# Memory values projected in the cross layers instead of beside the scans of the first mixers, in a two-model FP32 kernel on one core

## The chip, the cores and the metric

The kernel runs on one core of one Trainium2 chip. The metric is the device time of one execution in microseconds (us), the median of several runs. TensorE is called PE, VectorE DVE, ScalarE ACT, GpSimd POOL; SyncE, here SP, issues the DMA transfers of the main queue.

## The reference, cut to what matters

Two models of two layers each stand one behind the other, on 512 tokens of width 1024. In the first each layer is a mixer (attention beside a gated delta rule, which is scanned over chunks of 64 tokens in both directions) and a feed-forward block. In the second each layer is a mixer (even, odd), a cross attention to a memory of 256 rows, and a feed-forward block. The memory is an input and doesn't depend on the tokens:

```python
def _memory_cross_attention(h, mem_h, w_q, w_kv, q_norm_g, k_norm_g, w_o):
    q = _rms(_split_heads(h @ w_q, XA_HEADS), q_norm_g)          # 4 heads of 256
    mk, mv = _split_cols(mem_h @ w_kv, (XA_HEADS * XA_HD, XA_HEADS * XA_HD))
    mk = _rms(_split_heads(mk, XA_HEADS), k_norm_g)
    mv = _split_heads(mv, XA_HEADS)
    logits = jnp.einsum('bhqd,bhkd->bhqk', q, mk) * (XA_HD ** -0.5)
    p = jax.nn.softmax(logits, axis=-1)
    o = jnp.einsum('bhqk,bhkd->bhqd', p, mv)
    return _merge_heads(o) @ w_o

...
        x = x + _memory_cross_attention(_rms(x, xa_norm_g[l]), _rms(mem, xa_mem_norm_g[l]), ...)
```

`mem_h @ w_kv`, the keys and values of the memory, is what the change moves.

## The kernel before, in words

Ten phases follow each other: m0 f0 m1 f1 (the first model's mixers and feed-forward blocks), ev xa0 g0 od xa1 g1 (the second's mixers, cross attentions and feed-forward blocks). A framework with a scheduler takes the program as written and decides the order of the instructions on each engine; SP takes its transfers in that order, one behind another, and each waits on SP until its buffer is free or its data are there.

Every large product is made of three matmuls on split numbers: high part of the weights by high part of the activation (L491), high by low (L494), low by high (L495), in `proj`. Weights come by 1024 KB transfers (`fetch`, L465, two buffers `wraw`), and are split a piece at a time: ACT makes `whi` (L478), POOL `wlo` (L384, a line that all helpers' additions share).

The scan of a mixer (`scan`, `scan_step`) has 16 steps, which alternate between the two directions. A step is a chain: products with `kes` (L1202), an addition on DVE (`yv`), products with `invs`, a multiplication on DVE, products with `keys`, the new state `S` on DVE, and products with `outs` (L1236). The tiles `kes`, `keys`, `outs` come from DRAM in units that serve two steps (`load`, L1151 to L1154); `invs` come by `join` (L1161), which finishes the inverse blocks with two groups of matmuls (L1173, L1180) and copies on ACT (`offd`, L1165; `prod`).

Beside the scan runs side work, a chain of generators: first what is left of the gate logits (blocks of 24 matmuls of 512 columns), then `memory_kv(l, last)`, then the attention's output products. `side.beside(scan(), R3)` lets the scan do a step, which counts 4.0, and runs side work until its own count reaches R3 times the steps' count. Each half group of `memory_kv` counts 3 and is 24 matmuls of 256 columns; with R3 = 0.75 that is one half group a step. `memory_kv` of layer l (l = 0 in m0, 1 in m1) reads the memory, scales and splits it into four `act` tiles, and then for each of four heads projects the keys (two half groups, through `proj`) and the values (two half groups, L1677, L1680 and L1681), copies them on ACT and writes them to DRAM (`mkv`, eight transfers of 256 KB per layer, L1686). `issue_behind` lets such a block start only behind the scan's last L1236 matmul of that moment.

The cross layer (`_cross`) projects the queries of a head (`queries`: 48 matmuls of 512 columns), reads that head's keys and values back (`ahead`, L1722), norms the keys (a sum by L416, a spread over partitions by L459, `kn`), scales the values on ACT, and makes the logits (L1754 to L1756), the softmax and the products with the values (L1781 to L1783).

Of the kernel before, what the change touches and what calls it, by code (L numbers as in the profile page):

```python
# [251 lines left out]

R1, R2, R3, R4 = 0.6,1,0.75,0.6
G1, G2 = 0, 2
E1, E2 = 0,3

# [47 lines left out]
class Prog:  # L306
# [1337 lines left out]
    def memory_kv(self, l, last):  # L1644


        nc, M, wkv = self.nc, NMEM, self.A["xakv"][l]
        mem = self.fetch(self.A["mem"], 8, M)
        ma = []
        for k in range(8):  # L1650
            if k % 2 == 0:
                t = self.actp.tile([P, 2, 2, M], F32R, name="act", tag="act")
            a, g = t[:, k % 2], self.vec(f"xm{l}", k)
            nc.scalar.activation(a[:, 0], mem[:, k], AF.Copy, scale=g)
            nc.vector.scalar_tensor_tensor(a[:, 1], mem[:, k], g, a[:, 0].bitcast(F32), ALU.mult, ALU.subtract)
            ma.append(a)
        for h in range(4):
            for g in (h, 4 + h):
                ws = self.wload(wkv[g], 8, 256, rows=g > 3)
                t = self.nrm.tile([P, 2, M], F32, name="mkv", tag="nsq", bufs=2)  # L1660
                dst = self.dr.tile([P, 2, M], F32, name=f"mkv{l}{g}")
                self.mkv[l, g] = dst
                if g < 4:
                    for j in range(2):
                        ps = self.psb()[:, :M]
                        self.proj(ps, ws[j], ma, n=M, behind=last[-1] if last else None)
                        nc.scalar.copy(t[:, j], ps)
                        if j == 0:
                            yield 3
                else:  # L1670
                    pv = [self.psb()[:, :M] for _ in range(2)]
                    for i, (k0, hi, lo) in enumerate(ws[0]):
                        for j in range(2):
                            tok = slice(j * P, (j + 1) * P)
                            for k in range(2):
                                a = ma[k0 + k]
                                mm = nc.tensor.matmul(pv[j], a[:, 0, tok], hi[:, k], start=k0 + k == 0, stop=False)  # L1677
                                if last and k + j == 0 and i % 2 == 0:
                                    self.issue_behind(mm, last[-1])
                                nc.tensor.matmul(pv[j], a[:, 0, tok], lo[:, k], start=False, stop=False)  # L1680
                                nc.tensor.matmul(pv[j], a[:, 1, tok], hi[:, k], start=False, stop=k0 + k == 7)  # L1681
                        if i == 1:
                            yield 3
                    for j in range(2):
                        nc.scalar.copy(t[:, j], pv[j])
                nc.sync.dma_start(out=dst, in_=t)  # L1686
                yield 3

    def cross(self, l, nm, nxt):
        with self.phase("xa") as xp, self.banks(2, 2, 2):  # L1690
# [2 lines left out]
    def _cross(self, l, nm, nxt, xp):  # L1693
        nc, gs = self.nc, self.gs
        wq = self.A["xaq"][l]
        M = NMEM

        def roots(sq, scale, eps, n, r):

            self.tt(sq[0], sq[0], sq[1], ALU.add, "gpsimd")  # L1700
            return self.rs_cols([sq[0]], self.all_features, 1, scale, eps, nt=n // P, r=r)[0]

        def queries(h):

            qs, sqs = [], []
            for i, w in enumerate(self.wload(wq[h], 8, 256)):
                ps, q, sq, g = self.psb(), gs("qs", 4, (P, 2, S), F32R), gs("sq", 4), self.vec(f"xq{l}", i)
                self.proj(ps, w, nm.acts)
                nc.scalar.activation(q[:, 0], ps, AF.Copy, scale=g)
                nc.vector.scalar_tensor_tensor(q[:, 1], ps, g, q[:, 0].bitcast(F32), ALU.mult, ALU.subtract)  # L1710
                nc.scalar.activation(sq, ps, AF.Square)
                qs.append(q)
                sqs.append(sq)
            return qs, roots(sqs, 1.0, 256 * EPS, S, nm)


        mr = self.mem[l]
        q0 = queries(0)

        def ahead(g):  # L1720
            t = gs("mkv", 4, (P, 2, M))
            nc.sync.dma_start(out=t, in_=self.mkv[l, g])  # L1722
            return t

        ys = []
        for h in range(4):
            kr, vr = ahead(h), ahead(4 + h)
            kn, ks, sqs = [], [], []
            for j in range(2):
                x, sq = gs("kx", 3, (P, M)), gs("sq", 4)[:, :M]  # L1730
                nc.scalar.activation(x, kr[:, j], AF.Copy, scale=self.vec(f"xk{l}", j))
                nc.scalar.activation(sq, kr[:, j], AF.Square)
                ks.append(x)
                sqs.append(sq)
            ps = self.spread(roots(sqs, 1.0 / 256, EPS, M, mr), nt=2)[:, :M]
            for x in ks:
                self.tt(x, x, ps, ALU.mult)
                kn.append(gs("kn", 4, (P, 2, M), F32R))
                self.split(kn[-1], x)
            vt = [gs("vt", 4, (P, 2, M), F32R) for _ in range(2)]  # L1740
            for t in range(2):
                v = gs("kx", 3, (P, M))
                nc.scalar.activation(v, vr[:, t], AF.Copy, scale=mr.rc[:, t])
                self.split(vt[t], v, "gpsimd")
            qs, rq = q0 if h == 0 else queries(h)

            pT = [gs("pT", 3, (P, 2, S), F32R) for _ in range(2)]
            for q2 in range(2):
                ps = self.psf()
                for t in range(2):  # L1750
                    tk, o = slice((2 * q2 + t) * P, (2 * q2 + t) * P + P), ps[:, t * M:t * M + M]
                    for i in range(2):
                        a, b = qs[i], kn[i]
                        nc.tensor.matmul(o, a[:, 0, tk], b[:, 0], start=i == 0, stop=False)  # L1754
                        nc.tensor.matmul(o, a[:, 0, tk], b[:, 1], start=False, stop=False)  # L1755
                        nc.tensor.matmul(o, a[:, 1, tk], b[:, 0], start=False, stop=i == 1)  # L1756
                pt = self.psg()
                mx = xp.tile([P, 4], F32, name="mx", tag="mx", bufs=4)
                nc.vector.tensor_reduce(mx[:, 0:2], ps.rearrange("p (t m) -> p t m", t=2), AX.X, ALU.max, negate=True)
                pr = gs("pr", 2)  # L1760
                tq = rq[:, 2 * q2:2 * q2 + 2].rearrange("p t c -> p (t c)")
                self.tt(mx[:, 0:2], mx[:, 0:2], tq, ALU.mult)
                for t in range(2):
                    p = pr[:, t * M:t * M + M]
                    nc.scalar.activation(p, ps[:, t * M:t * M + M], AF.Exp, bias=mx[:, t:t + 1], scale=tq[:, t:t + 1],
                                         accum_out=mx[:, 2 + t:3 + t])
                nc.vector.reciprocal(mx[:, 2:4], mx[:, 2:4])
                for t in range(2):
                    p = pr[:, t * M:t * M + M]
                    nc.vector.tensor_scalar(p, p, mx[:, 2 + t:3 + t], None, ALU.mult)  # L1770
                    for k in range(2):
                        nc.tensor.transpose(pt[:, (2 * k + t) * P:(2 * k + t + 1) * P], p[:, k * P:(k + 1) * P], self.ident)  # L1772
                pv = pt.rearrange("p (k t) -> p k t", k=2)
                tk = slice(q2 * 256, q2 * 256 + 256)
                nc.scalar.copy(pT[0][:, :, tk], pv)
                self.tt(pT[1][:, :, tk], pv, pT[0][:, :, tk].bitcast(F32), ALU.subtract)
            for i in range(2):
                po = self.psg()
                c = slice(i * P, i * P + P)
                for k in range(2):  # L1780
                    nc.tensor.matmul(po, vt[k][:, 0, c], pT[0][:, k], start=k == 0, stop=False)  # L1781
                    nc.tensor.matmul(po, vt[k][:, 1, c], pT[0][:, k], start=False, stop=False)  # L1782
                    nc.tensor.matmul(po, vt[k][:, 0, c], pT[1][:, k], start=False, stop=k == 1)  # L1783
                y = xp.tile([P, 2, S], F32R, name=f"y{2 * h + i}")
                self.split(y, po)
                ys.append(y)
        self.out_proj(self.A["xao"][l], ys[:4], nxt, final=False)
        self.out_proj(self.A["xao"][l], ys[4:], nxt, 4)
# [45 lines left out]
```

## Time and profile before

| | |
|---|---|
| median of 3 runs | 3359.07 us (3357.63 to 3361.22) |
| the profiled execution's own time | 3360.63 us |
| its span in the trace | 3358.8 us |
| PE busy | 3211.1 us, 96% of the span |
| DVE, ACT, POOL busy | 54%, 45%, 51% |
| mean granted TensorE clock | 0.987 of full speed |
| scans of the mixers | about 344 to 450 us and 1250 to 1356 us |
| first parts of the cross layers | about 2137 to 2182 us and 2880 to 2920 us |

PE busy is the engine that nearly always works. The 147.6 us in which it doesn't lie in a few stages, the two scans and the starts of the cross layers among them. A line of the trace's order shows start, length, engine, source line, operation, output and inputs; what stands in square brackets is the idle time of the engine just before the instruction, and what ended it.

### The profile page before, as it was taken

The page shows a single profiled execution, that of the slowest core. Times are in us where ns is not written, and L with a number is a line of the kernel's source. Part 1 is how long each engine was busy: PE and PEld are TensorE (multiplying, and loading weights), DVE is VectorE, ACT ScalarE, POOL GpSimd, SP SyncE. Part 2 cuts the span into 40 slices and gives each one's busy share as a digit, 9 for nine tenths or more (in the row PEclk, how much of TensorE's full clock was granted, in tenths as well). Part 3 has the DMA queues.
Part 4 walks back from the last instruction along what each step waited for, and adds up shares of the span by engine and source line. Part 5 has one row for each costly group of instructions (what it writes and reads, how often), then busy time and mean ns, then how long its engine had stood idle before and what let it go on. Part 6 is the DMA issues. An engine that isn't in the chain of part 4 may idle for free. (4 is left out here: it accounts for less than half of the span.)

```text
span 3358.8 us, 47110 instructions
## 1 busy us (share of the span) xinstructions
PE 3211.1 (96%) x17342; PEld 2647.7 (79%) x17342; DVE 1822.8 (54%) x3549; ACT 1512.8 (45%) x2836; POOL 1721.8 (51%) x1453
## 2 busy tenths in 40 slices
PE   8988899999998898999999999899999999999999
PEld 6767787888886677878888777687888888888887
DVE  7687444734476964456445667673232476653222
ACT  5646544433455555344334433554343444644332
POOL 4542466444545334755445555645555533555554
PEclk9999999999999999999999999999999999999999
DMA  4632643222337236422222211323222221222222
GB/s 156 175 98 65 171 142 122 96 101 101 115 110 198 82 92 179 140 100 97 92 101 104 86 63 51 101 75 119 103 101 88 100 81 59 97 90 92 99 101 88
DMA packets 142301, 355.13 MB, mean 106 GB/s; under 512 B 44111, under 2 KB 81359, under 8 KB 113144
## 3 DMA queue, kind: packets, MB, share of 16 engines
q1 hardware_dynamic: 140640, 348.63, 32.4%
q10 hardware_dynamic: 1432, 3.49, 0.4%
q8 instruction: 138, 2.26, 0.3%
q14 instruction: 91, 0.75, 0.1%
HBM read 318.44 MB, written 34.16 MB: 105 GB/s over the span
## 5 line engine op out<-in xcount | busy, mean ns | idle before, releaser
L384 POOL TENSOR_TENSOR wlo<-wraw,whi 128x512 fp32r<-128x512 f32 (+2 forms) x1044 | 1353.4, 1299 | 1412.7 <-ACT whi L478 1359.4
L478 ACT CAST whi<-wraw 128x512 fp32r<-128x512 f32 (+2 forms) x1044 | 633.1, 608 | 1120.8 <-PE psb L494 816.6
L491 PE MATMUL psb<-act,whi 128*128 128x512 f32 (+1 forms) x2016 | 788.5, 392 | 26.0 <-ACT whi L478 12.7
L495 PE MATMUL psb<-act,wlo 128*128 128x512 f32 (+1 forms) x2016 | 782.8, 389 | 0.8 <-POOL wlo L384 0.6
L494 PE MATMUL psb<-act,whi 128*128 128x512 f32 (+1 forms) x2016 | 782.7, 388 | 0.6 <-DVE act L277 0.6
L491 PEld LDWEIGHTS psb<-act,whi 128*128 128x128 f32 x2016 | 383.4, 190 | 105.2 <-ACT whi L478 14.6
L495 PEld LDWEIGHTS psb<-act,wlo 128*128 128x128 f32 x2016 | 382.6, 190 | 76.5 <-POOL wlo L384 2.8
L494 PEld LDWEIGHTS psb<-act,whi 128*128 128x128 f32 x2016 | 383.3, 190 | 74.4 <-DVE act L277 1.9
L384 DVE TENSOR_TENSOR x<-psb,x 128x512 f32<-128x512 f32 x168 | 115.2, 689 | 372.5 <-PE psb L495 372.1
L491 PE MATMUL ps<-act,whi 128*128 128x512 f32 (+1 forms) x720 | 282.4, 392 | 3.4 <-ACT rB L303 3.4
L494 PE MATMUL ps<-act,whi 128*128 128x512 f32 (+1 forms) x720 | 281.8, 391 | 0.0
L495 PE MATMUL ps<-act,wlo 128*128 128x512 f32 (+1 forms) x720 | 281.4, 391 | 0.0
L491 PE MATMUL psb<-mid,whi 128*128 128x512 f32 x704 | 276.5, 394 | 1.0 <-DVE x L384 1.0
L495 PE MATMUL psb<-mid,wlo 128*128 128x512 f32 x704 | 276.2, 392 | 0.0
L494 PE MATMUL psb<-mid,whi 128*128 128x512 f32 x704 | 273.7, 389 | 0.0
L491 PEld LDWEIGHTS ps<-act,whi 128*128 128x128 f32 (+1 forms) x720 | 134.8, 187 | 34.2 <-ACT rB L303 4.7
L495 PEld LDWEIGHTS ps<-act,wlo 128*128 128x128 f32 (+1 forms) x720 | 134.9, 187 | 29.7
L494 PEld LDWEIGHTS ps<-act,whi 128*128 128x128 f32 (+1 forms) x720 | 134.9, 187 | 29.4
L495 PEld LDWEIGHTS psb<-mid,wlo 128*128 128x128 f32 x704 | 132.2, 188 | 30.3
L491 PEld LDWEIGHTS psb<-mid,whi 128*128 128x128 f32 x704 | 132.3, 188 | 29.4 <-DVE x L384 1.5
L494 PEld LDWEIGHTS psb<-mid,whi 128*128 128x128 f32 x704 | 132.1, 188 | 29.6
L384 DVE TENSOR_TENSOR cv<-ps,cv 128x512 f32<-128x512 f32 (+1 forms) x60 | 41.5, 692 | 187.9 <-PE ps L495 106.5
(427 smaller groups left out, 5268.1 us busy)
## 6 DMA issues: line engine op xcount, KB each, us to landing
wraw<-in_wup SPq DMA_DIRECT2D x44, 1024.0 KB, 4.8
wraw<-in_fup SPq DMA_DIRECT2D x44, 1024.0 KB, 4.9
wraw<-in_win SPq DMA_DIRECT2D x38, 1024.0 KB, 5.1
wraw<-in_xakv SPq DMA_DIRECT2D x16, 1024.0 KB, 7.1
wraw<-in_wdn SPq DMA_DIRECT2D x16, 1024.0 KB, 4.8
wraw<-in_evin SPq DMA_DIRECT2D x16, 1024.0 KB, 4.8
wraw<-in_fdn SPq DMA_DIRECT2D x16, 1024.0 KB, 4.9
wraw<-in_odin SPq DMA_DIRECT2D x12, 1024.0 KB, 4.8
```

The lines of the kernel that those rows point to most:

```text
L384: getattr(self.nc, eng).tensor_tensor(out, a, b, op)
L478: nc.scalar.copy(hi, part)
L491: mm = nc.tensor.matmul(ps, hi[:, i], acts[k][:, 0, :n], start=k == 0, stop=False)
L494: nc.tensor.matmul(ps, hi[:, i], acts[k][:, 1, :n], start=False, stop=False)
L495: nc.tensor.matmul(ps, lo[:, i], acts[k][:, 0, :n], start=False, stop=k == kc - 1)
```

## The change

R3 falls from 0.75 to 0.375, so that a half group stands at every second step, and `memory_kv` makes only the keys: 8 half groups of 24 matmuls per layer in place of 16. The four split tiles of the memory, which it made already, are also written to DRAM (`mact`, 4 times 512 KB per layer). The cross layer reads these four tiles back, and for each head fetches and splits the value weights (1024 KB) and makes the 48 value matmuls there, into two PSUM banks, from which ACT takes them with the scale. The values' way through DRAM (4 writes and 4 reads of 256 KB per layer) and their 8 ACT copies per layer are gone.

```diff
-R1, R2, R3, R4 = 0.6,1,0.75,0.6
+R1, R2, R3, R4 = 0.6,1,0.375,0.6
@@ memory_kv
+        self.mkv[l] = parts = self.dr.tile([4, P, 2, 2, M], F32, name=f"mact{l}")
...
             ma.append(a)
+            if k % 2:
+                nc.sync.dma_start(out=parts[k // 2], in_=t.bitcast(F32))
         for h in range(4):
-            for g in (h, 4 + h):
-                ws = self.wload(wkv[g], 8, 256, rows=g > 3)
...
-                else:
-                    pv = [self.psb()[:, :M] for _ in range(2)]
-                    for i, (k0, hi, lo) in enumerate(ws[0]):
-                        for j in range(2):
...
-                    for j in range(2):
-                        nc.scalar.copy(t[:, j], pv[j])
-                nc.sync.dma_start(out=dst, in_=t)
-                yield 3
+            ws = self.wload(wkv[h], 8, 256)
+            t = self.nrm.tile([P, 2, M], F32, name="mkv", tag="nsq", bufs=2)
+            self.mkv[l, h] = dst = self.dr.tile([P, 2, M], F32, name=f"mkv{l}{h}")
+            for j in range(2):
+                ps = self.psb()[:, :M]
+                self.proj(ps, ws[j], ma, n=M, behind=last[-1] if last else None)
+                nc.scalar.copy(t[:, j], ps)
+                if j == 0:
+                    yield 3
+            nc.sync.dma_start(out=dst, in_=t)
+            yield 3
@@ _cross
         mr = self.mem[l]
+        wkv = self.A["xakv"][l]
+        mt = [gs("mact", 4, (P, 2, 2, M), F32R) for k in range(4)]
+        for k in range(4):
+            nc.sync.dma_start(out=mt[k].bitcast(F32), in_=self.mkv[l][k])
+        ma = [mt[k // 2][:, k % 2] for k in range(8)]
         q0 = queries(0)
...
-            kr, vr = ahead(h), ahead(4 + h)
+            kr = ahead(h)
...
+            ws = self.wload(wkv[4 + h], 8, 256, rows=True)
             vt = [gs("vt", 4, (P, 2, M), F32R) for _ in range(2)]
+            pv = [self.psb() for _ in range(2)]
             for t in range(2):
+                tok = slice(t * P, (t + 1) * P)
+                o = pv[t][:, :M]
+                for k, hi, lo in ws[0]:
+                    for i in range(2):
+                        nc.tensor.matmul(o, ma[k + i][:, 0, tok], hi[:, i], start=k + i == 0, stop=False)
+                        nc.tensor.matmul(o, ma[k + i][:, 0, tok], lo[:, i], start=False, stop=False)
+                        nc.tensor.matmul(o, ma[k + i][:, 1, tok], hi[:, i], start=False, stop=k + i == 7)
                 v = gs("kx", 3, (P, M))
-                nc.scalar.activation(v, vr[:, t], AF.Copy, scale=mr.rc[:, t])
+                nc.scalar.activation(v, o, AF.Copy, scale=mr.rc[:, t])
```

What the scheduler makes of it is seen in the engines' order. On PE in the scan of m0 a step with a half group behind it stood so before (the four groups of a step, then the first two of the half group's 24 matmuls):

```order
L1202 MATMUL ps_3833<-yv,invs_3247 64x64 x8
L1202 MATMUL ps_3896<-S,kes_3243 64x64 x8
L1202 MATMUL ps_3848<-yv,keys_3246 64x64 x8
L1236 MATMUL ps_3858<-sv_3819,outs_3251 64x64 x8
L491 MATMUL psb<-act,whi 128x256
L494 MATMUL psb<-act,whi 128x256
```

After the change there is at this place (behind the last block of gate logits) no block for four steps:

```order
L1202 MATMUL ps_3814<-yv,invs_3249 64x64 x8
L1202 MATMUL ps_3889<-S,kes_3244 64x64 x8
L1202 MATMUL ps_3829<-yv,keys_3245 64x64 x8
L1236 MATMUL ps_3839<-sv_3800,outs_3250 64x64 x8
L1202 MATMUL ps_3902<-yv,invs_3247 64x64 x8
L1202 MATMUL ps_3975<-S,kes_3243 64x64 x8
L1202 MATMUL ps_3917<-yv,keys_3246 64x64 x8
L1236 MATMUL ps_3927<-sv_3888,outs_3251 64x64 x8
```

Over the whole scan 11 half groups stood between steps and 5 behind the last step; now 4 stand between steps, one in two steps, and 4 behind the last. The third block of gate logits stands two steps later than before.

On SP in the same scan, behind the loads of the fourth unit, there stood before, with the units' loads around two fetches of memory weights:

```order
L1161 DMA invs_3248<-ti_198 64x8x64 x2
L465 DMA wraw<-in_xakv 128x2048
L1154 DMA keys_3246<-scrK 64x4x128
L1152 DMA outs_3251<-dnscr 128x8x128
L1154 DMA keys_3246<-scrK 64x4x128
L465 DMA wraw<-in_xakv 128x2048
L1151 DMA kes_3243<-dnscr 64x4x128 x2
```

and now:

```order
L1161 DMA invs_3248<-ti_198 64x8x64 x2
L1659 DMA mact_4025<-act 128x1024 x4
L465 DMA wraw<-in_xakv 128x2048
L1151 DMA kes_3243<-dnscr 64x4x128 x2
L465 DMA wraw<-in_xakv 128x2048
L1161 DMA invs_3249<-ti_201 64x8x64 x2
L1151 DMA kes_3244<-dnscr 64x4x128
```

The four writes of the memory's tiles and the first weight fetch stand ahead of the fifth unit's `kes`; the second fetch stands ahead of the next `invs`.

On PE in cross layer 0 the last query matmul was followed by the keys' spread (L459) and the logits (L1754, with `kn` the normed keys and `qs` the queries):

```order
L495 MATMUL psb<-act,wlo 128x512
L459 MATMUL ps_19740<-cstt,rc 128x128 x2
L416 MATMUL ps_19856<-cstt,sq 128x128 x2
L1754 MATMUL ps_19763<-kn,qs 128x256
```

and now there are 96 value matmuls of the heads 0 and 1 (L1737 to L1739 in the changed kernel) ahead of that spread, of which these are the last two (L1752 is now the first line of the logits):

```order
L1738 MATMUL psb<-wlo,mact 128x256
L1739 MATMUL psb<-whi,mact 128x256
L459 MATMUL ps_19172<-cstt,rc 128x128 x2
L416 MATMUL ps_19354<-cstt,sq 128x128 x2
L1752 MATMUL ps_19263<-kn,qs 128x256
```

The values of heads 2 and 3 stand between the later logits and query products. In cross layer 1 it is alike. In m1, ahead of the scan, the scheduler's order changes too, with no edit there: 21 projection matmuls of 512 columns more (141 in place of 120) stand ahead of the last transposes (L864) that feed the inversion (`solve`).

## Rows read from the trace of the kernel before

**Rows 1.** Page, busy time of the engines: span, and PE's busy time.

```profile
span 3358.8 us, 47110 instructions
PE 3211.1 (96%) x17342; PEld 2647.7 (79%) x17342; DVE 1822.8 (54%) x3549; ACT 1512.8 (45%) x2836; POOL 1721.8 (51%) x1453
```

**Rows 2.** Scans by stretch: length, busy by engine, then clock, DMA share, GB/s.

```profile
core 0: us, PE busy (x) PEld busy (x) DVE busy (x) ACT busy (x) POOL busy (x), PEclk, DMA share, GB/s
344.00:380.00 36.00, 30.81 (x483) 26.44 (x484) 20.23 (x50) 21.28 (x52) 12.66 (x21) 0.91 0.58 160
357.00:364.20 7.20, 5.38 (x146) 4.66 (x144) 5.84 (x15) 2.33 (x5) 1.90 (x2) 1.00 0.22 58
380.00:410.00 30.00, 26.28 (x449) 23.58 (x447) 11.25 (x30) 15.20 (x37) 14.57 (x18) 1.00 0.72 185
...
1250.00:1286.00 36.00, 29.42 (x492) 24.68 (x492) 20.47 (x51) 22.64 (x57) 13.56 (x22) 1.00 0.61 168
```

**Rows 3.** PE in order of time, m0's scan, a step without a block.

```profile
360.01 0.69 PE L1202 MATMUL ps<-yv,keys 128*64 128x64 f32 x16 [1.22 <-DVE yv L384]
...
362.62 0.69 PE L1202 MATMUL ps<-yv,keys 128*64 128x64 f32 x16
363.60 0.69 PE L1236 MATMUL ps<-sv,outs 128*64 128x64 f32 x16 [0.29 <-DVE sv L384]
```

**Rows 4.** PE in order of time, m0's scan, a step with a half group.

```profile
386.10 0.69 PE L1236 MATMUL ps<-sv,outs 128*64 128x64 f32 x16 [0.25 <-PE ps L1202]
386.71 0.38 PE L491 MATMUL psb<-act,whi 128*128 128x256 f32 x1
...
389.56 0.28 PE L495 MATMUL psb<-act,wlo 128*128 128x256 f32 x1
389.77 0.69 PE L1202 MATMUL ps<-yv,invs 128*64 128x64 f32 x16
...
391.99 0.69 PE L1236 MATMUL ps<-sv,outs 128*64 128x64 f32 x16 [0.30 <-DVE sv L384]
```

**Rows 5.** PE in order of time, m0's scan, the wait for a late inverse block.

```profile
406.31 0.69 PE L1173 MATMUL ps<-invs,offd 128*64 128x64 f32 x16 [2.83 <-ACT offd L1165]
```

**Rows 6.** DMA issues, 340 to 460 us: transfer, count, KB each, us to landing.

```profile
wraw<-in_xakv SPq DMA_DIRECT2D x8, 1024.0 KB, 8.3
outs<-dnscr SPq DMA_DIRECT2D x6, 512.0 KB, 6.6
mkv<-mkv SPq DMA_DIRECT2D x7, 256.0 KB, 2.0
```

**Rows 7.** DMA issues of the whole span, from the page: an undisturbed weight fetch.

```profile
wraw<-in_wup SPq DMA_DIRECT2D x44, 1024.0 KB, 4.8
```

**Rows 8.** Cross layers by stretch, columns as in the scans.

```profile
2137.00:2160.00 23.00, 22.95 (x108) 19.05 (x108) 11.79 (x22) 15.60 (x32) 21.02 (x18) 1.00 0.50 165
2160.00:2182.00 22.00, 18.11 (x95) 15.29 (x94) 14.58 (x63) 12.47 (x30) 10.07 (x10) 0.95 0.23 72
...
2900.00:2920.00 20.00, 17.86 (x100) 15.31 (x99) 15.79 (x68) 12.46 (x31) 7.28 (x7) 0.91 0.17 52
```

**Rows 9.** Waits in cross layer 0: us in total, times, longest.

```profile
PE ps L459 <- DVE rc L384: 2.7, 1, 2.7
```

**Rows 10.** Line 384, 2130 to 2185 us: pieces of low weights on POOL, ns min/median/max.

```profile
L384 POOL TENSOR_TENSOR wlo<-wraw,whi x17: 1189/1290/1743, 2131.7 to 2172.7; 128x512 fp32r<-128x512 f32 x16, 128x256 fp32r<-128x256 f32 x1
```

**Rows 11.** SP in order of time, cross layer 0: the reads of keys and values.

```profile
2137.13 1.75 SPq L1722 DMA_DIRECT2D mkv<-mkv  x4
2143.93 0.33 SPq L465 DMA_DIRECT2D wraw<-in_xaq  x1
```

**Rows 12.** Mixer m1 ahead of its scan, by stretch, around the inversion.

```profile
1050.00:1110.00 60.00, 46.82 (x205) 37.34 (x204) 37.13 (x69) 21.00 (x40) 26.47 (x22) 0.89 0.64 172
1110.00:1170.00 60.00, 51.42 (x249) 39.91 (x248) 55.36 (x113) 32.84 (x64) 21.17 (x15) 0.97 0.35 93
```

**Rows 13.** Waits in m1, 1020 to 1175 us: us in total, times, longest.

```profile
PE ps L416 <- ACT cv L884: 7.5, 1, 7.5
```

**Rows 14.** A stretch of f0 with nothing but matmuls of 512 columns on PE.

```profile
540.00:560.00 20.00, 20.00 (x88) 16.05 (x87) 6.26 (x8) 9.34 (x15) 13.56 (x22) 1.00 0.21 76
```

More of the change, by code (lines that the diff above doesn't have):

```diff
@@ L1656, in memory_kv @@
             ma.append(a)
+            if k % 2:
+                nc.sync.dma_start(out=parts[k // 2], in_=t.bitcast(F32))
         for h in range(4):
-            for g in (h, 4 + h):
-                ws = self.wload(wkv[g], 8, 256, rows=g > 3)
[L1660 to L1663, printed above, removed]
-                    for j in range(2):
[L1665 to L1668, printed above, removed]
-                            yield 3
-                else:
-                    pv = [self.psb()[:, :M] for _ in range(2)]
-                    for i, (k0, hi, lo) in enumerate(ws[0]):
-                        for j in range(2):
[L1674 to L1684, printed above, removed]
-                        nc.scalar.copy(t[:, j], pv[j])
-                nc.sync.dma_start(out=dst, in_=t)
-                yield 3
@@ L1717, in _cross @@
         mr = self.mem[l]
+        wkv = self.A["xakv"][l]
[3 more added lines that the diff above has]
+        ma = [mt[k // 2][:, k % 2] for k in range(8)]
         q0 = queries(0)
         def ahead(g):
-            t = gs("mkv", 4, (P, 2, M))
+            t = gs("mkv", 2, (P, 2, M))
             nc.sync.dma_start(out=t, in_=self.mkv[l, g])
```

## The prediction

> **What bounds the kernel now.** I begin with the page: PE is busy for 3211.1 of 3358.8 us [rows 1]. The reader should see that 147.6 us are all that can be won by better order, and that the 384 value matmuls which the change moves (192 per layer) are neither saved nor added. So the question is only how much PE time is idle or slow around them, in the place that they leave and in the place to which they go.
>
> The second view is the scans by stretch [rows 2]. From 344 to 380 us PE is idle for 5.2 of 36 us, and from 380 to 410 for 3.7 of 30, although side work stands between the steps. In the second scan the first stretch has 6.6 us idle. So the scan's stretches are bound neither by PE alone nor by the chain of steps alone. They also carry the heaviest transfers: a DMA share of 0.58 and 0.72.
>
> The third is PE in order of time there. Without a block, one step follows the other after 362.62 − 360.01 = 2.61 us [rows 3], with waits for DVE in it. With a half group it takes from one L1236 to the next 391.99 − 386.10 = 5.89 us [rows 4]. The 24 matmuls themselves run at (389.56 − 386.71) / 23 = 0.124 us [rows 4].
>
> The fourth is the cross layers by stretch [rows 8]. From 2137 to 2160 us PE is full; from 2160 to 2182 it is busy for 18.11 of 22 us at a clock of 0.95; from 2900 to 2920 for 17.86 of 20 us at 0.91. The chain there is short: the norm of the keys, whose result PE awaits for 2.7 us [rows 9]. Nothing else is ready for PE then. This is the idle time that the value matmuls can fill.
>
> **The change part by part.** The sum is made against the profiled execution's 3360.63 us, which is 1.6 above the median of 3359.07; I carry the differences over to the median.
>
> *Half groups out of the scan.* Between steps stood 11 half groups, now 4: seven fewer per scan, and one fewer behind the last step. A step that loses its half group falls from 5.89 to 2.61 us [rows 3, 4], 3.28 us less; the same 24 matmuls cost 24 × 0.124 = 2.98 us elsewhere. So a half group leaves 0.30 us of friction behind, 2.1 us per scan and **−4.2 us** for both. The half group behind the last step costs the same in either place: 0. This holds only if the steps that are left bare really run at 2.61 us, for which the tiles of the units must have landed; that is the next term.
>
> *Transfers in the scan.* At 5.89 us a step the loads of the next unit had twice the time that bare steps give them. Ahead of the fifth unit's `kes` SP now issues four `mact` writes and a weight fetch, and behind it a second fetch ahead of `invs`. What is queued there: the loads of the fifth unit, for which the products with `kes` wait, behind those all later products of that direction, since the state is a chain. A weight fetch takes 8.3 us to land among the scan's transfers, and a unit's `outs` 6.6 us [rows 6]. The four writes are 2 MB, as much as two weight fetches, which undisturbed take 4.8 us each [rows 7]: 9.6 us per scan is the upper bound, if all of it shows. The lower bound is 0, since four weight fetches per layer and four `mkv` writes leave the scan, 5 MB against 2 MB added. Between them I take the nearest thing that the trace shows: one late `invs`, through its copy on ACT, stops PE for 2.83 us [rows 5]. One more such wait per scan: **+5.6 us** (0 to 19.2). A gain is excluded here beyond the friction, because the chain is not faster than its 2.61 us.
>
> *The clock in bare steps.* The stretch from 344 to 380 us ran at a mean clock of 0.91, the one from 1250 at 1.00 [rows 2]: a loss of 36 × 0.09 = 3.2 us in the one, nothing in the other. A piece of bare steps, 357 to 364.2 us, with PE busy for 5.38 of 7.20 us, ran at 1.00 [rows 2]. Four bare steps follow each other now, 10.4 us. I take half of the 9% of it, 0.5 us each: **+0.9 us** (from −3.2, if the first scan's spell goes, to +6.5). The Trainium skill, "TensorE: Matmul & The Clock Gate", section "HAM oscillation — how this bites in real kernels", says that idle gaps between groups of matmuls bring the clock down and that work after them then runs slowly. It speaks against this change; the piece of bare steps doesn't bear it out, and by the rule alone the sum would be that of the third rival.
>
> *Values in the cross layers.* The 96 matmuls of the first two heads stand exactly ahead of the spread for which PE waits. They are 96 × 0.124 = 11.9 us of work, longer than the idle time there. Idle and clock give back at most 22 − 18.11 + 22 × 0.05 = 5.0 us in layer 0 and 20 − 17.86 + 20 × 0.09 = 3.9 us in layer 1 [rows 8], together −8.9 us. Against it stand the weights. The two heads' values are 8 pieces of `wlo`, 8 × 1.29 = 10.3 us of POOL [rows 10], where POOL was already busy for 21.02 of 23 us up to 2160 and for 10.07 of 22 behind it [rows 8]. That is 41.4 us of POOL in 45 + 11.9 us: it fits, with little slack at the start. The reads also double, from four `mkv` tiles ahead of the first logits, which were issued at 2137.13 us [rows 11], to 2 MB of `mact`, with two weight fetches behind. If this cover is missing, PE waits for a piece as long as it now waits for the norm, 2.7 us [rows 9], up to 7.5 in each layer if the reads come wholly late (the 8.3 us of a crowded fetch [rows 6] less what the queries cover). I take 1.5 us each, the middle between nothing and 2.7: −8.9 + 3.0 = **−5.9 us** (−8.9 to +6). The values of heads 2 and 3 stand among full stretches: 0.
>
> *The order in m1 ahead of the scan.* Nothing is edited there, but 21 matmuls of 512 columns move ahead of the transposes that feed the inversion. One takes 20 / 88 = 0.227 us [rows 14], so the inversion may start 4.8 us later. PE is idle there for 13.2 us from 1050 to 1110 and for 8.6 us from 1110 to 1170 [rows 12], of which 7.5 us are one wait for ACT [rows 13]. So either the 21 matmuls only fill idle time (up to −4.8), or they push a chain on DVE, which is busy for 55.36 of 60 us [rows 12], back by as much (+4.8). I take **+1.5 us**, nearer to the push, because that chain is what the later idle time waits for.
>
> The sum: −4.2 + 5.6 + 0.9 − 5.9 + 1.5 = **−2.1 us**, 3358.5 us for an execution like the profiled one, **3357.0 us** as median. A measurement of this kernel can tell about 0.2%, 6.7 us, from no change: it is the same, with a lean to faster. The likeliest case by itself spans some 3351 to 3364 us.
>
> **The rivals.** *Faster: the bare steps find their data.* Then the transfers cost nothing and the cross layers give back all their idle time: −4.2 − 8.9 = −13.1 us, 3346.0 us. For it speaks that 5 MB leave the scans against 2 MB, and that the bare steps before [rows 3] waited for no transfer. Against it: in these the loads had been made ahead, at the scan's start. Chance 0.28.
>
> *Slower: the writes stand in the way of the fifth unit.* The mechanism is at one place: `mact` ahead of `kes` on SP. It decides if `kes` and `outs` of the fifth unit land later than the two bare steps ahead of them take, 5.2 us; `outs` alone takes 6.6 us among crowded transfers [rows 6]. If the writes show wholly, the sum is −4.2 + 19.2 + 0.9 − 5.9 + 1.5 = +11.5 us, 3370.6 us. For it speaks the wait that a late `invs` causes already [rows 5]. Against it: the writes are made early in the side work, and may be through while the gate logits' third block runs. Chance 0.14. The Trainium skill, "DMA: Bandwidth & Descriptors", section "Queues, rings and completion order", says that each DMA engine takes descriptors in ring order, so that small loads issued behind large ones wait for these. The late landings among crowded transfers agree; the rule makes this rival possible, not certain.
>
> *The clock falls in the bare steps.* If two spells like that of 344 to 380 us come in each scan, 4 × 3.2 = 12.8 us [rows 2] stand in place of 0.9: −2.1 + 11.9 = +9.8 us, 3368.9 us. For it speaks that PE has more gaps; against it the piece at clock 1.00. Chance 0.08.
>
> **How the numbers follow.** The forecast has 0.50. Faster by over 0.2%: nearly all of the first rival, 0.28, and 0.07 of the forecast, where the inversion and the clock fall well: 0.35. Slower: the second rival's 0.14, half of the third's, 0.04, and 0.03 of the forecast: 0.21. The same: 0.44. The range reaches from a little under the first rival's 3346.0 to a little above the second's 3370.6, 3342 to 3372 us; beyond it lie only sums of several bounds.
>
> **What would show it.** In the profile of the changed kernel: bare steps in the scans at about 2.6 us, no wait of PE over 3 us for `kes`, `keys` or `outs`, a granted clock of at least 0.95 from 360 to 400 us, value matmuls at 0.118 to 0.124 us each, and no wait for the keys' spread in the starts of the cross layers. The prediction is wrong if PE there waits for POOL's value pieces or for `mact`, if a product with `kes` waits for a transfer in the second half of the scans, if whole stretches of the scans run at half clock, or if the stretch of the inversion in m1 changes by more than 5 us.

## The result, and the profile of the changed kernel

The changed kernel takes 3384.21 us (median of 4 runs, 3381.54 to 3388.58), the kernel before 3359.03: a ratio of 1.0073, 95% interval 1.0061 to 1.0086. It is slower by 25.2 us; the forecast was 3357.0 us, the range 3342 to 3372.

The page first, which answers to [rows 1]:

```profile
span 3383.6 us, 47090 instructions
PE 3215.2 (95%) x17342; PEld 2656.5 (79%) x17342; DVE 1831.8 (54%) x3549; ACT 1506.0 (45%) x2820; POOL 1719.1 (51%) x1453
```

PE has the same 17342 matmuls and is busy for 4 us more; the other 21 us of the longer span are idle time. To see where it lies, I cut the program at instructions that both traces have: the first product with `kes` in each scan, the first addition behind each mixer's output projection (L546), the last L1382 of ev, the first convolution of g0 and g1, the last L1604 of od. So the stage up to `kes` of m1 has f0 in it, od has g0, and the rest is g1. Lengths of the stages against those of before, in us (other kernels of the study stand below for later):

| kernel | to first `kes` | scan m0 to L546 | to `kes` of m1 | scan m1 to L546 | f1, ev | cross 0 | od | cross 1 | rest | span |
|---|---|---|---|---|---|---|---|---|---|---|
| changed | +0.2 | −8.3 | −2.8 | −6.8 | −1.6 | +24.3 | −0.1 | +19.8 | +0.1 | +24.8 |
| e1 R3 alone | −2.9 | +9.2 | −1.6 | +8.6 | −1.3 | −2.2 | +1.6 | −0.3 | +0.1 | +11.2 |
| e15 bare, no fetch | −8.1 | +15.3 | −4.6 | +21.1 | −0.4 | −2.6 | −1.6 | −0.2 | +0.1 | +19.0 |
| e7 late writes | 0.0 | −14.4 | −2.9 | −12.9 | −1.1 | +22.6 | −0.9 | +20.2 | 0.0 | +10.6 |
| e4 double writes | −3.0 | −7.3 | −2.0 | −8.6 | −1.3 | +21.4 | +1.1 | +19.8 | +0.1 | +20.2 |
| e16 no `kes` reload | −1.9 | −21.9 | −2.9 | −19.4 | −2.5 | +20.9 | +2.2 | +19.8 | +0.1 | −5.6 |
| e5 dense, early | +1.5 | −17.9 | −5.5 | −15.9 | −1.8 | +23.9 | 0.0 | +19.8 | +0.1 | +4.2 |
| e9 dense, late | −1.3 | −14.6 | −3.1 | −16.7 | −1.7 | +21.5 | +2.9 | +19.8 | +0.1 | +6.9 |
| e13 middle, late | −2.4 | −18.2 | −6.6 | −20.3 | +1.3 | +23.0 | +0.1 | +19.8 | +0.1 | −3.2 |
| e12 dense, queries first | −2.4 | −19.0 | −2.5 | −18.0 | −1.7 | +13.9 | −1.0 | +18.2 | +0.1 | −12.4 |
| e19 changed, queries first | −3.1 | −9.4 | −1.4 | −11.4 | −1.9 | +15.9 | +1.1 | +18.2 | +0.1 | +8.1 |
| e17 middle, queries first | +0.5 | −20.4 | −5.9 | −22.4 | −2.9 | +14.8 | −1.6 | +18.3 | +0.1 | −19.5 |
| e18 before, R3 in the middle | −1.9 | +5.1 | −0.6 | +1.6 | +1.5 | −1.5 | +1.3 | −1.6 | 0.0 | +3.9 |

The first column tells what one profile is worth: what stands there is edited in none of these, and it moves by up to 3 us (in e15 a block of gate logits has left it). The third, up to `kes` of m1, isn't edited either, and it is shorter by 0.6 to 6.6 us in all of them. I read no single stage's difference under 3 us, and one under 7 only where both scans, both layers or another run show it too.

By the prediction's price of 2.98 us for a half group, 23.8 us of work leave each scan. The changed kernel's scans are only 8.3 and 6.8 us shorter: **32.5 us are lost there**. The cross layers take up 24.3 and 19.8 us, 3.5 less than the 47.6 us of work that came. So the loss is in the scans. By stretch, to hold against [rows 2]:

```profile
380.00:410.00 30.00, 18.59 (x322) 16.68 (x321) 12.55 (x29) 10.89 (x28) 7.22 (x12) 0.77 0.95 217
...
1250.00:1286.00 36.00, 27.11 (x511) 23.23 (x511) 21.72 (x52) 17.10 (x42) 9.92 (x16) 0.91 0.61 167
```

From 380 to 410 us PE is busy for 18.6 us of 30 (26.3 before), the granted clock has fallen from 1.00 to 0.77, and the DMA share is 0.95 in place of 0.72. The waits of PE from 340 to 470 us say for what:

```profile
PE ps L1202 <- DMA kes<-dnscr: 9.3, 4, 3.9
PE ps L1202 <- DVE yv L384: 5.6, 6, 1.5
...
PE ps L1236 <- DMA outs<-dnscr: 1.2, 1, 1.2
```

Before, the longest line of this kind was for DVE (3.3 us), and none was for a transfer. On PE in order of time the waits stand where the bare steps are, the first ahead of the third block of gate logits (375.55 to 381.4 us), the others behind it:

```profile
372.80 1.01 PE L1202 MATMUL ps<-S,kes 128*64 128x64 f32 x13 [2.77 <-DMA kes<-dnscr]
...
392.79 0.40 PE L1202 MATMUL ps<-S,kes 128*64 128x64 f32 x2 [2.35 <-DMA kes<-dnscr]
...
400.75 0.34 PE L1202 MATMUL ps<-S,kes 128*64 128x64 f32 x1 [3.94 <-DMA kes<-dnscr]
...
404.73 1.12 PE L1236 MATMUL ps<-sv,outs 128*64 128x64 f32 x16 [1.22 <-DMA outs<-dnscr]
```

Each direction of the scan has one `kes` tile (`kes[d]` in `load`), so the load of a unit can go out only behind the last product with the unit before it, and its own first product comes two steps later. A unit's `kes` is two transfers. On SP the `kes` behind the later waits were issued long before they landed:

```profile
378.34 6.09 SPq L1659 DMA_DIRECT2D mact<-act  x4
384.49 0.42 SPq L465 DMA_DIRECT2D wraw<-in_xakv  x1
385.00 1.44 SPq L1151 DMA_DIRECT2D kes<-dnscr  x2
386.54 0.64 SPq L465 DMA_DIRECT2D wraw<-in_xakv  x1
...
388.99 0.70 SPq L1151 DMA_DIRECT2D kes<-dnscr  x1
389.78 3.49 SPq L1154 DMA_DIRECT2D keys<-scrK  x1
...
394.02 4.58 SPq L1154 DMA_DIRECT2D keys<-scrK  x1
398.65 0.60 SPq L1151 DMA_DIRECT2D kes<-dnscr  x1
```

The wait of 2.77 us ends at 372.80, ahead of the four writes at 378.34: they can't be its cause. The `kes` at 388.99 is used at 400.75, 11.8 us later. The view of the tile `kes` from 375 to 412 us has its time from issue to landing; the first line is the changed kernel, the second the kernel before:

```profile
DMA to landing us min/median/max: 7.4/7.6/11.6
```

```profile
DMA to landing us min/median/max: 2.6/3.4/4.2
```

A transfer of 128 KB lands 7.6 us after its issue (median) where it took 3.4. Like for like, the fifth unit's two, issued at 385.0 us, land after 7.6 us where those issued at 385.1 before took 2.6.

In cross layer 0 PE still waits, in the changed kernel's waits from 2095 to 2286 us:

```profile
PE ps L459 <- DVE rc L384: 3.8, 1, 3.8
...
PE psb L1737 <- ACT sq L1695: 2.3, 1, 2.3
```

The wait for the keys' spread has not been filled (2.7 us in [rows 9]); it is 3.8, and 2.3 us ahead of the first value matmul have come to it.

### The profile page after: what moved, and what is told of

It is laid out like the page before. It is cut to its first block, busy times and chain, and to the rows that moved or that the text cites. A ratio compares the mean times of both kernels' runs of the same rounds, so it can differ in the third digit from the quotient of the medians.

```text
span 3383.6 us, 47090 instructions
## 1 busy us (share of the span) xinstructions
PE 3215.2 (95%) x17342; PEld 2656.5 (79%) x17342; DVE 1831.8 (54%) x3549; ACT 1506.0 (45%) x2820; POOL 1719.1 (51%) x1453
## 3 DMA queue, kind: packets, MB, share of 16 engines
q10 hardware_dynamic: 1432, 3.49, 0.4%
```

## The experiments

Two theories at first: **W**, the four writes of the memory's tiles ahead of the loads are the cause; **B**, the bare steps use up the units faster than transfers bring them, whatever is written. All times are medians; "before" is the kernel before on the same chip in the same series. It moved by 2.2 us from series to series (3357.26 to 3359.44); the changed kernel's 3384.21 is from the first series alone, so differences against it are good to some 2 us.

**e1, R3 alone, on the kernel before.**

```diff
-R1, R2, R3, R4 = 0.6,1,0.75,0.6
+R1, R2, R3, R4 = 0.6,1,0.375,0.6
```

> The kernel before with R3 = 0.375 alone: keys and values both stay beside and behind the scans, no memory tiles are written, the cross layers are those of before. The steps of the scan are as bare as in the changed kernel. Theory W (the four writes of the memory's tiles, ahead of the weight fetches and the fifth unit's kes on SP, make the scan late): about 3357 us, -4 to +4 against before, PE waits for kes under 3 us per scan. Theory B (bare steps use up the units faster than the transfers bring them, whatever is written): the loss of the scans stays, some +25 us, about 3384 us, with PE waits for kes of about 9 us per scan and a clock under 0.8 from 390 to 410 us.

Measured: 3371.72 us against 3358.28, ratio 1.0044 (1.0029 to 1.0059). PE's waits from 340 to 470 us:

```profile
PE ps L1202 <- DMA kes<-dnscr: 7.1, 2, 3.8
```

This lies between the two theories: bare steps alone cost 13 us, with no work moved and no memory tiles written. Theory W by itself falls, and B explains half of the loss.

**e7, late writes, on the changed kernel.**

```diff
-        ma = []
+        ma, tiles = [], []
...
             if k % 2:
-                nc.sync.dma_start(out=parts[k // 2], in_=t.bitcast(F32))
+                tiles.append(t)
...
+        for k in range(4):
+            d = nc.sync.dma_start(out=parts[k], in_=tiles[k].bitcast(F32))
+            self.issue_behind(d, last[-1])
```

> The changed kernel with the four writes of the memory's tiles moved behind the scan on SP; the same bytes, the same bare steps. Theory W: the scans' loss of some 28 us goes, 3355 to 3360 us. Theory B: nothing changes much, 3378 to 3386 us.

Measured: 3371.6 us against 3358.28, ratio 1.0042 (1.0025 to 1.0059): 12.6 us less than the changed kernel. In the table the scans become 6.1 us shorter each. Both theories hold a part. `kes` lands after 6.4 us (median, 375 to 412 us) and PE waits for it for 6.9 us in m0's scan:

```profile
PE ps L1202 <- DMA kes<-dnscr: 6.9, 2, 3.7
```

SP issues the fifth unit's `kes` at 384.7 us here and at 385.0 in the changed kernel, and they land after 5.6 us and 7.6. So for this unit the writes don't hold SP; they hold the transfers that are issued behind them. The next unit's loads are later in the changed kernel on both counts: its first `kes`, issued at 388.5 us here and 389.0 there, lands after 8.2 us here and 11.6 there, and its second is issued at 394.1 here and 398.7 there. SP is busy for 2.85 us here with the `keys` ahead of that one, and for 4.58 there:

```profile
391.24 2.85 SPq L1154 DMA_DIRECT2D keys<-scrK  x1
394.14 1.16 SPq L1151 DMA_DIRECT2D kes<-dnscr  x1
```

**e5 and e9, a block at every step, with early and with late writes.** R3 = 0.75 in the changed kernel (e5), and in e7 (e9).

> The changed kernel with R3 = 0.75: keys alone at every step, so that a half group (and behind the keys the attention's output products) covers every step; the writes stay early, ahead of the fourth unit's tiles. Theory W: still 15 us or more lost, 3370 to 3385 us. Theory B: the scans are as before or better, 3350 to 3358 us.

> The changed kernel with R3 = 0.75 and the writes behind the scan. Both theories: no late kes, 3348 to 3356 us, of which some -4 us come from the starts of the cross layers. If it is not faster than before, values in the cross layers cost as much there as they leave free in the scans.

Measured: e5 3363.55 us (1.0017, 1.0007 to 1.0027), e9 3366.51 us (1.0020, 1.0010 to 1.0029), before 3358.28. With every step covered there is no wait of PE for `kes` in either scan, and early writes cost nothing that shows: they cost time only where the steps are bare. So W needs B. But both are slower than before, by 5 and 8 us, where I had expected a gain: 16.3 us of the scans' 47.6 are still lost in e9, of which the runs show only a part (below, e13), and the cross layers cost 41.3 us.

**e15, all steps bare, and no fetch among the units' loads.** The kernel before with R3 = 0.

> The kernel before with R3 = 0: all side work (the third block of gate logits, keys, values, output products) stands behind the scan, so that all its steps are bare, and no weight fetch and no write is issued between the units' loads after the fourth unit; the cross layers are those of before. Two theories are left for the 15 us that R3 alone cost in the two scans. Theory F (the weight fetches just ahead of the fifth unit's kes make it late; bare steps by themselves lose little): PE waits for kes under 2 us per scan, the sum of both scans within 6 us of before, 3355 to 3365 us. Theory B (bare steps outrun the units' own loads): waits for kes, keys and outs of 6 us or more per scan although nothing else is in the queue, and 10 us or more lost, above 3369 us.

Measured: 3378.15 us against 3357.26, ratio 1.0066 (1.0049 to 1.0083). Theory F falls. In m0's scan PE waits for `kes` three times, although SP issues nothing but the units' own loads from 351 us on:

```profile
366.31 1.01 PE L1202 MATMUL ps<-S,kes 128*64 128x64 f32 x13 [3.80 <-DMA kes<-dnscr]
...
383.55 1.01 PE L1202 MATMUL ps<-S,kes 128*64 128x64 f32 x13 [3.72 <-DMA kes<-dnscr]
...
400.35 1.01 PE L1202 MATMUL ps<-S,kes 128*64 128x64 f32 x13 [2.20 <-DMA kes<-dnscr]
```

The `kes` behind the first two, issued at 358.91 and 377.12 us, land after 7.3 and 6.4 us, with the units' own `outs` (512 KB) and `keys` issued just ahead of them. In m1's scan of the same kernel the late tile is another, the inverse blocks, by way of their copy on ACT (10.6 us in 5 waits of PE; ACT itself waits for these tiles' transfers for 16.3 us). Bare steps outrun the units' own loads.

**e4, each tile written twice.**

```diff
+        more = self.dr.tile([4, P, 2, 2, M], F32, name=f"mbct{l}")
...
                 nc.sync.dma_start(out=parts[k // 2], in_=t.bitcast(F32))
+                nc.sync.dma_start(out=more[k // 2], in_=t.bitcast(F32))
```

> The changed kernel with each of the four tiles of the memory written twice, to two places in DRAM, at the same point of SP's queue. If the writes' place and bytes ahead of kes are what the late-writes kernel saved (some 6 us in each scan), the second set costs about as much again: 3392 to 3400 us. If it was the wait of SP for the split tiles alone, the second set adds next to nothing: 3382 to 3388 us.

Measured: 3381.76 us against 3357.26, ratio 1.0080 (1.0065 to 1.0095), like the changed kernel. This doesn't tell what I meant it to: with eight writes the scheduler put the fifth unit's `kes` ahead of the two weight fetches. It shows only that twice the bytes, with the order changed so, are no worse. How the 12 us divide between the writes' bytes and the place of the fetches stays open.

**e16, `kes` loaded for the first two units alone.** The changed kernel without the later loads of `kes`; it leaves out this part of the recurrence's input.

```diff
-            for h, a in enumerate(half):
+            for h, a in enumerate(half if u < 2 else ()):
                 nc.sync.dma_start(out=kes[d][a, :, h], in_=dn[d, a, :, 0, c])
```

> The changed kernel, early writes and sparse steps kept, without the loads of kes from the third unit on; this leaves out that part of the recurrence's input, so the output isn't the reference's, while the instructions of PE, DVE, ACT and POOL stay. If the landing of kes into its single buffer is what the changed scans lose, at least 12 of the 31 us that they lose come back, 3372 us or less. If outs, keys or invs are as late behind the writes and fetches and only take over, less than 6 us come back, 3378 us or more.

Measured: 3356.01 us against 3359.44, ratio 0.9994 (0.9984 to 1.0003): 28 us less than the changed kernel. The scans lose 6.3 us in place of 32.5, with writes, fetches and bare steps as they were, and what PE waits for in m0 is DVE again (in m1 one wait for `keys`, 2.9 us, is left). Its waits from 340 to 470 us, first two lines:

```profile
PE ps L1202 <- DVE yv L384: 6.4, 7, 1.4
PE ps L1180 <- ACT prod L1176: 2.6, 6, 1.0
```

So the late `kes` is the cause of up to 26 of the 32.5 us, the fall of the clock behind its waits included. The edit also takes 12 transfers of 128 KB per scan off the queue; how much of the 26 us is theirs was not separated. A second `kes` tile per direction, which would let the loads go out earlier, was not tried.

**e13 and e18, R3 = 0.5625**, with e7's late writes (e13) and in the kernel before (e18).

> The changed kernel with the writes behind the scan and R3 = 0.5625, between the sparse (0.375, 3371.6 us) and the dense one (0.75, 3366.5 us). If bare steps are what the sparse one loses, it lies between or near the dense one, 3364 to 3370 us; if the dense one loses because its side work is used up before the scan's tail, this one is better than both, 3358 to 3363 us.

> The kernel before with R3 = 0.5625 alone, values in the scans. If the better spread of the side work over steps, not the place of the values, is what made the middle kernel fast, this is 5 us or more faster than before, under 3353 us; if every block beside a step pays, it is slower than before by a few us, 3360 to 3366 us.

Measured: e13 3353.81 us against 3357.26, ratio 0.9988 (0.9978 to 0.9997); e18 3360.65 against 3359.44, ratio 1.0008 (0.9999 to 1.0017). Three half groups for four steps, with keys alone, are better than both neighbours: from the first half group on bare steps are single, and more of the attention's output products are left behind the scan, where PE is idle for 0.6 us in m0 at a clock of 1.00 and in e9 for 2.8 us at 0.94. This is a part only: of the 10.1 us between the profiles of e13 and e9, 7.2 lie in the two scan columns, the rest in stages that both kernels have alike. In the kernel before the same R3 changes nothing that can be told.

**e12 and e19, the next head's queries ahead of a head's values**, in e9 (e12) and in the changed kernel (e19).

```diff
+            qs, rq = q0
+            if h < 3:
+                q0 = queries(h + 1)
             ws = self.wload(wkv[4 + h], 8, 256, rows=True)
...
-            qs, rq = q0 if h == 0 else queries(h)
```

> The dense kernel with late writes, and in the cross layers the queries of the next head fetched and projected ahead of a head's values. If the starts of the cross layers lose their fill because value weights (48 matmuls of 256 columns per fetch) displace query weights (48 of 512 columns per fetch) in the two weight buffers, the wait for the keys' spread in cross layer 0 falls below 2 us and the layer costs 20 to 22 us more than before in place of 21.5 to 24; 3362 to 3365 us. If it is the norm's chain itself, no change: 3366 to 3368 us.

> The changed kernel, scans untouched, with the queries of the next head projected ahead of a head's values in the cross layers. If that order is what let the dense kernel's cross layers fall by 9 us, it gives the same here whatever the scans do: 3373 to 3377 us. If the two places share the gain, less: 3379 us or more.

Measured: e12 3351.65 us against 3357.26, ratio 0.9988 (0.9979 to 0.9997); e19 3370.14 against 3359.44, ratio 1.0038 (1.0025 to 1.0052), 14 us less than the changed kernel. Cross layer 0 costs 13.9 and 15.9 us more than before, where it cost 21.5 and 24.3; layer 1 18.2 in place of 19.8. That is more than I expected. The cross layers of e19 are 10.0 us shorter than the changed kernel's, those of e12 9.2 shorter than e9's; the rest of the 14 and 15 us lies in stages that the edit doesn't touch. The waits for the spread and for the first value matmul are gone in e12, and 0.6 us of the first is left in e19. SP in the changed kernel shows what the order does to the fetches, from 2107 us:

```profile
2107.04 0.33 SPq L465 DMA_DIRECT2D wraw<-in_xaq  x1
2113.48 0.33 SPq L465 DMA_DIRECT2D wraw<-in_xakv  x1
...
2124.02 0.33 SPq L465 DMA_DIRECT2D wraw<-in_xakv  x1
2131.00 0.33 SPq L465 DMA_DIRECT2D wraw<-in_xaq  x1
```

and in e19 from 2099:

```profile
2099.14 6.76 SPq L465 DMA_DIRECT2D wraw<-in_xaq  x2
...
2116.12 0.33 SPq L465 DMA_DIRECT2D wraw<-in_xakv  x1
2122.33 0.33 SPq L465 DMA_DIRECT2D wraw<-in_xaq  x1
```

In the changed kernel two value fetches go ahead of the second query fetch. A fetch of 1024 KB brings PE 48 matmuls of 512 columns for queries, 10.9 us, and 48 of 256 columns for values, 5.7 us. The runs show that the order matters; that it matters for this reason is my reading.

**e17, both: late writes, R3 = 0.5625, queries first.**

> Writes behind the scan, R3 = 0.5625 and the next head's queries first. If the gains of the two single edits (12.7 us for R3 against the dense kernel, 14.9 for the queries) lie in different places and add, about 3341 to 3346 us; if the dense kernel's profile shares part of them, 3347 to 3352 us, no better than one alone.

Measured: 3342.65 us (3339.15 to 3343.17) against 3359.44, ratio 0.9954 (0.9941 to 0.9966): the two gains add (against the kernel before of its own series e9 has +8.2 us, e13 −3.5, e12 −5.6, which makes −17.3; measured −16.8). It is faster than both kernels. How much of this comes from the values' place isn't shown: "queries first" was not run in the kernel before. The first line of its page, and its two scans by stretch (clock 0.98):

```profile
span 3339.3 us, 47070 instructions
```

```profile
358.70:444.10 85.40, 71.97 (x1280) 64.96 (x1274) 43.62 (x110) 41.63 (x99) 36.17 (x46) 0.98 0.57 151
1237.80:1321.20 83.40, 71.52 (x1277) 64.74 (x1274) 43.81 (x110) 41.66 (x99) 36.15 (x46) 0.98 0.58 154
```

## Why the prediction was wrong

*Half groups out of the scan, −4.2 us.* This step failed. It took 2.61 us for every bare step from one place [rows 3], where the first units had been loaded ahead, and said so as a condition. e1 and e15 show that the condition doesn't hold: bare steps cost 13 and 21 us with no work moved, and in m0 PE waits for `kes` for 7.1 and 9.7 us. The half group between two steps was no friction; it was the time in which the next unit landed.

*Transfers in the scan, +5.6 us, at most 19.2.* Right in place, far too small: together with the term above and the clock's, 32.5 us were lost where +2.3 had been reckoned. The bound was worked out from the bytes of the writes alone, as if without them no load were late; but the first wait for `kes` in m0, 2.77 us, stands ahead of the writes, and in e7, without them, 6.9 us are left. e7 shows that the writes in the changed kernel are worth some 12 us, e16 that `kes` carries up to 26. The second rival named the mechanism and its condition (two bare steps, 5.2 us, against the landing of `kes`); the landing took 7.6 us. Its 3370.6 us rested on the same bound, and so my range ended too low. The rule of the Trainium skill named there, "DMA: Bandwidth & Descriptors", section "Queues, rings and completion order", that each DMA engine takes descriptors in ring order, agrees with the trace: the fifth unit's `kes`, issued at 384.7 to 385.1 us in all three, lands after 2.6 us before, 5.6 in e7 behind a weight fetch and 7.6 in the changed kernel behind the writes too. I had given this rival 0.14.

*The clock, +0.9 us.* It fell to 0.77 from 380 to 410 us, a loss of at most 7 us in that stretch (30 us times what the granted clock lacks to 1; for a part of it PE waited), but behind waits of 2.35 and 3.94 us for `kes`, not by bare steps as such. From the first `kes` product to the last L1236 of m0, the changed kernel's line first and then that of e16, which has the same bare steps and no such waits:

```profile
358.40:444.20 85.80, 63.83 (x1181) 57.18 (x1178) 43.56 (x110) 35.89 (x87) 25.89 (x38) 0.90 0.65 159
```

```profile
356.30:428.50 72.20, 59.59 (x1181) 52.95 (x1178) 42.29 (x110) 36.00 (x87) 25.84 (x38) 0.98 0.60 167
```

Reckoned the same way, the clock loses at most 8.6 us and 1.4; in m1, at 0.88 and 0.95, 10.5 and 3.7. The third rival's effect came, as a result of the second's.

*Cross layers, −5.9 us.* They gave −3.5. Against the price of 23.8 us a layer, layer 1 gave −4.0 and layer 0 +0.5. The two layers before:

```profile
2114.60:2280.50 165.90, 152.31 (x725) 124.36 (x725) 110.35 (x291) 91.89 (x189) 93.63 (x83) 0.95 0.28 96
2848.70:3006.40 157.70, 153.90 (x752) 127.84 (x752) 99.43 (x274) 90.25 (x186) 91.33 (x80) 0.99 0.26 87
```

and in the changed kernel:

```profile
2095.30:2285.50 190.20, 174.43 (x917) 147.03 (x916) 111.45 (x291) 100.53 (x205) 112.84 (x99) 0.96 0.32 111
2853.60:3031.10 177.50, 175.32 (x944) 149.36 (x944) 107.11 (x273) 98.81 (x202) 112.53 (x96) 1.00 0.31 107
```

In layer 1 PE's idle time fell from 3.8 us to 2.2; the rest of the gain is that PE got busier by 21.4 us only, at a clock of 1.00 after 0.99. In layer 0 the idle time was not filled, it grew from 13.6 us to 15.8. The step that failed is that value matmuls come on top of the queries' fill; with two weight buffers they came in its place, at half the matmul time per fetch. e12 and e19, which change this order alone, take 7.6 and 8.4 us off layer 0. The bound of 7.5 us a layer for late reads was worked out from no row; PE waited for no `mact` there.

*The order in m1, +1.5 us.* The stage up to `kes` of m1, with f0 in it, became 2.8 us shorter. That is within what one profile varies, and no run was made for it.

*What held:* the value matmuls cost in the cross layers about what they were priced at (PE busier by 22.1 and 21.4 us, priced 23.8), and m1's reordering doesn't decide.

## What to carry to other kernels

Work that stands between the steps of a recurrence is cover for the loads of the next step; before taking it out, compare the bare step's time with the landing of those loads at the worst place of the queue, not with one step whose data were there already. Bulk transfers in the same queue cost nothing that showed while steps were covered (e5 against e9) and some 12 us where they were bare (e7), so where cover is taken out of a loop, move them behind it. To fill idle time while weights are fetched, try first the product with the most matmul time per byte of weights; here that order took 8 us off a layer.

## What was not expected of the hardware

A transfer of 128 KB lands after 3.4 us or after 11.6, depending on what was issued shortly ahead of it: the 11.6 us are of the one behind two fetches of 1024 KB and four writes of 512 KB, and without the writes (e7) its like took 8.2. SP's issues took longer, too: two of `keys`, which before took 0.6 to 0.7 us each, took 3.49 and 4.58 there. And the clock can go down in a stretch in which PE waits for 2 to 4 us at a time: 0.77 as a mean over 30 us with 18.6 us of work.
